# A two-block transformer step on one core: weight tiles split on VectorE alone, and TensorE multiplying zeros before its first inputs

## The chip, the cores and the metric

The kernel runs on one NeuronCore of a Trainium2 chip. The metric is the device time of one execution in microseconds (us). Five engines work side by side, each through its own queue in order: TensorE (PE in the profile; its weight loads are PEld), VectorE (DVE), ScalarE (ACT), GpSimd (POOL) and SyncE (SP, which here only starts transfers). DMA queues move data between HBM and the on-chip memory SBUF. TensorE writes to the accumulation memory PSUM.

## The reference

Two blocks follow one another on 256 rows of 1024 float32 values. All products are float32.

```python
# block 1
xn = rms_norm(x, norm1_g);  proj = xn @ w_in              # gates, keys, queries, values
mixed = concat(hgrn2_mixer(...), gla_mixer(...))          # two gated linear attentions
h = x + mixed @ w_out
h = h + peer_ffn(rms_norm(h, norm2_g), ...)               # 8 heads x 16 experts of 16384, gathered by row
x = rms_norm(h, norm_f_g)
# block 2
h = rms_norm(x, norm_pre);  cols = h @ w_in_2
ys = [deltanet(...), spatial_gating(...), sliding_window(...), memory(...)]
merged = sum(sigmoid(gate_n) * (ys[n] @ w_up[n]) for n in range(4))
out = x + rms_norm(merged @ w_out_2, norm_post)
```

## The kernel before

The 256 rows are two blocks of 128 partitions, handled as `b` = 0 and 1. The program is one long order written out in Python: generators yield between small steps, and `run`, `weave` and `pace` interleave them. Every engine then works through its own queue in the order in which the generators issued the instructions.

**Weights.** They come from HBM as tiles of 128 x 1024 float32 (512 KB), numbered `i`; four tiles make a group `g` of 512 output columns. `load_to` starts the transfers on SP in that order into `slot` tiles, of which there are 28 for all purposes. `wt(g, c)` loads some tiles ahead (`depth`) and cuts some tiles ahead (`ahead`) of the one that TensorE is about to use.

**Split products.** Most groups (`SPLIT`) are multiplied in three products of float32r halves (`mm3`, lines 365 to 367): high by high, high by low, low by high. So each tile is cut first (`cut`, lines 216 and 217): ScalarE casts it to the high half `hi`, then `lo = x - hi` is subtracted on VectorE or on Pool. Inputs are cut too, always on VectorE. The high and low halves lie in `pair` tiles (`wp`), of which there are 6 in the front and in the tail; a few of the last group are in `wh` and `wl`. `cut_to` chooses the engine of a weight tile: Pool if `state["pool"]` is set and `i % state["share"] == 0`, else VectorE; `share` is 2 at first, 3 in the front after the first inputs, 2 (`SHARE`) in the tail. Between front and tail `pool` is False.

**Stages.** In the front, `norm1` scales, transposes and cuts the input of both blocks (its steps are interleaved by hand with the cuts of the first four tiles), `bounds` computes small constants, and `front_chan`, `front_v` and `front_gate` project (hf, glow, hq, gq, gk, vg, g). `mixer_levels` works out the scores of the linear attention in seven levels on VectorE and TensorE (lv), woven between the projections; `mixer_out`, `peer_norm` and `first_scores` follow, and the first experts are selected. Then 256 gathers of 1 MB by Pool bring the experts' rows, VectorE and TensorE use them, and the rest of block 1 and a part of block 2 run in their shadow. In the tail, `tail_main` projects the second block's branches (zgm, zsw, zxm, zdn), gates and merges, while `pace` hands out the steps of `deltanet`, `sliding`, `spatial` and `memory_attn` between them; `finish` projects once more (o), normalizes and stores. L1468 and L1469 are the two VectorE operations of `merge`, L1190 and L1222 belong to the triangular solve of `deltanet`, L1353 to L1362 to the softmax of `sliding`.

**PSUM.** `bank` hands out accumulation tiles from rings of three, one ring ("pj") for projections and one ("ps") for the rest.

The edit touches `cut_to` and the hand-written order at the start:

```python
    n0, n1 = norm1(0), norm1(1)
    for g, n in ((n0, 0), (n1, 0), (n0, 0), (n1, 1), (n0, 1), (n1, 2), (n0, 3), (n1, 4)):
        next(g, None)
        cut_to(n)
```

Of the kernel before, what the change touches and what calls it, by code (L numbers as in the profile page):

```python
# [11 lines left out]
BF = mybir.dt.bfloat16  # L12
# [7 lines left out]
P = 128  # L20
# [7 lines left out]
N_SLOT, N_PAIR = 28, 6  # L28
N_EARLY, N_LATE = 8, 4
SLOT_US = 2.7  # L30
ZW = 7.0
SHARE, AH, LAST = 2, 2, 4
SC_OF = (0, 1, 2, 3, 4, 6, 5, 7)
LEVELS = (1, 2, 4, 8, 16, 32, 64)

# [22 lines left out]
def run(*gens):  # L58

    live = list(gens)  # L60
    while live:
        for g in list(live):
            try:
                next(g)
            except StopIteration:
                live.remove(g)
# [75 lines left out]
def kernel(ctx, tc, I, out, dbg=None):  # L142
    nc = tc.nc
    dbg = dbg or {}
    V, S, G, TE = nc.vector, nc.scalar, nc.gpsimd, nc.tensor
# [10 lines left out]
    def slot(name, dt=F32):  # L156

        return big.tile([P, 1024], dt, tag="slot", name=name)
# [11 lines left out]
    def pair(name, dt=F32):  # L170

        k = turn["at"] % turn["ring"]
        turn["at"] += 1
        return (pairs if k < N_PAIR else late["pairs"]).tile([P, 2048], dt, tag="pair", name=name)
# [19 lines left out]


    raw, parts = {}, {}
    state = {"next": 0, "cut": 0, "depth": 8, "ahead": N_PAIR - 2, "share": 2}

    def is_split(i):
        return any(4 * a <= i < 4 * b for a, b in SPLIT)  # L200

    def chunks(t):
        return t.rearrange("p (c n) -> p c n", c=2)
# [11 lines left out]
    def cut(x, hi, lo, eng=None):  # L215
        S.copy(hi, x)  # L216
        (eng or V).tensor_tensor(out=lo, in0=x, in1=hi.bitcast(F32), op=OP.subtract)  # L217

    def cut_to(n, eng=None):
        for i in range(state["cut"], min(n, state["next"])):  # L220
            if is_split(i):
                if i // 4 in (Z_GU, G_O2 + 1):
                    hi, lo = slot(f"wh{i}", F32R), slot(f"wl{i}", F32R)
                else:
                    wp = pair(f"wp{i}", F32R)
                    hi, lo = wp[:, :1024], wp[:, 1024:]
                cut(raw[i], hi, lo, eng or (G if state["pool"] and i % state["share"] == 0 else V))
                parts[i] = chunks(hi), chunks(lo)
        state["cut"] = max(state["cut"], min(n, state["next"]))

    def wt(g, c):
        i = 4 * g + c // 2
        load_to(i + 1 + state["depth"])
        cut_to(i + 1 + state["ahead"])
        return chunks(raw[i])[:, c % 2]
# [35 lines left out]
    S.activation(warm, one, AF.Exp)  # L271
    mhalf = cpool.tile([P, 1], F32, name="mhalf")
    V.memset(mhalf, -0.5)
    iota16 = cpool.tile([P, 16], BF, name="iota16")
    G.iota(iota16, pattern=[[1, 16]], base=0, channel_multiplier=0, allow_small_or_imprecise_dtypes=True)


    def bank(name, tag="pj"):
        return psum.tile([P, 512], F32, tag=tag, name=name)
# [4 lines left out]
    def small(name, *shape, dt=F32, bufs=2):  # L284
        return work.tile([P, *shape], dt, tag=name, name=name, bufs=bufs)
# [31 lines left out]
    def rstd2(ss):  # L317

        t = small("rst2", 2)
        V.tensor_scalar(t[:, 0:1], ss[:, 0:1], ss[:, 1:2], EPS, op0=OP.add, op1=OP.add)  # L320
        G.tensor_tensor(out=t[:, 1:2], in0=t[:, 0:1], in1=mhalf, op=OP.pow)
        return t[:, 1:2]

    def halves_rstd(x, junk, adds, meanwhile=lambda: None):

        ss = small("ssh", 2)
        for nh in range(2):
            s = slice(nh * 512, (nh + 1) * 512)
            adds[nh](s)
            S.activation(junk[:, s], x[:, s], AF.Square, scale=D ** -0.5, accum_out=ss[:, nh:nh + 1])  # L330
        r = rstd2(ss)
        meanwhile()
        return r

    def transposed(x, put, n=KC, scale=None):

        for h in range(n // 4):
            pt = bank4("pt")
            for c in range(4):
                cc = 4 * h + c  # L340
                if scale is None:
                    TE.transpose(pt[:, c], x[:, cc * P:(cc + 1) * P], ident)  # L342
                else:
                    TE.matmul(pt[:, c], x[:, cc * P:(cc + 1) * P], scale, start=True, stop=True)
            pe(1.1)
            yield
            put(h, pt)
        yield
# [10 lines left out]
    def gained(o, pt, gain, h):  # L359
        V.tensor_tensor(out=o, in0=pt, in1=gain[:, 4 * h:4 * h + 4, None].to_broadcast([P, 4, P]), op=OP.mult)  # L360
# [33 lines left out]
    def scaled(x, name):  # L394

        xs = slot(f"{name}_s")
        r = row_rstd(x, D, name, xs)
        V.tensor_scalar(xs, x, r, None, op0=OP.mult)
        return xs
# [6 lines left out]
    def norm1(b):  # L406
        tb = slice(b * P, (b + 1) * P)

        def put(h, pt):
            t = xT[b][:, 4 * h:4 * h + 4]  # L410
            if b == 0:
                gained(t, pt, chan[:, C_N1:C_N1 + 8], h)
            else:
                for c in range(4):
                    S.activation(t[:, c], pt[:, c], AF.Copy, scale=chan[:, C_N1 + 4 * h + c:C_N1 + 4 * h + c + 1])
            cut(t, xh[h][:, :, tb], xl[h][:, :, tb])

        xs = scaled(xr[b], f"n1{b}")
        yield
        yield from transposed(xs, put)  # L420
# [17 lines left out]
    def bounds():  # L438
        V.tensor_tensor(out=lb[:, 0], in0=l0, in1=l1, op=OP.max)
        V.tensor_tensor(out=lb[:, 1], in0=l0, in1=lb[:, 0], op=OP.subtract)  # L440
        V.tensor_tensor(out=lb[:, 2], in0=l1, in1=lb[:, 0], op=OP.subtract)
        S.activation(lb[:, 1:3], lb[:, 1:3], AF.Exp)
        V.tensor_tensor(out=lb[:, 3], in0=lb[:, 1], in1=lb[:, 2], op=OP.add)
        V.reciprocal(lb[:, 4], lb[:, 3])
        V.tensor_tensor(out=fb, in0=lb[:, 2], in1=lb[:, 4], op=OP.mult)
        V.tensor_scalar(fb, fb, 0.5, None, op0=OP.mult)
        V.tensor_tensor(out=fa, in0=lb[:, 1], in1=lb[:, 4], op=OP.mult)
        V.tensor_tensor(out=fa, in0=fa, in1=fb, op=OP.add)
        V.tensor_scalar(nfb, fb, -1.0, None, op0=OP.mult)
        cut(w_glow, gls[0], gls[1])  # L450
# [397 lines left out]
    def peer():  # L848
# [5 lines left out]
        for i in range(n + AHEAD[1] + LAG[1]):  # L854
# [38 lines left out]
            if n - 10 <= i < n - 2 and i % 2 == 0:  # L893
                cut_to(4 * Z_GU + 1 + (i - n + 10) // 2, V)
                load_to(4 * Z_GV + (i - n + 8) // 2)
# [28 lines left out]
    def last_out(b):  # L924

        x, junk, a, nf = xr[b], hn[b], acc[b], rowt["nf"]

        def add(s):
            V.tensor_tensor(out=x[:, s], in0=x[:, s], in1=a.rearrange("p a n -> p (a n)")[:, s], op=OP.add)

        def scale(s):
            V.scalar_tensor_tensor(x[:, s], x[:, s], r, nf[:, s], op0=OP.mult, op1=OP.mult)

        r = halves_rstd(x, junk, (add, add))
        yield
        r2 = halves_rstd(x, junk, (scale, scale))
        dump("x2", x, lambda d: d[b * P:(b + 1) * P])
        dr = small("dg", P, bufs=3)
        V.tensor_scalar(dr, ident, r2, None, op0=OP.mult)
        yield  # L940
        hT[b] = slot3(f"hT{b}", 8)
        hh2[b] = slot3(f"hh{b}", 8, P, F32R), slot3(f"hl{b}", 8, P, F32R)

        def put(h, pt):
            s = slice(4 * h, 4 * h + 4)
            gained(hT[b][:, s], pt, chan[:, C_NP:C_NP + 8], h)
            cut(hT[b][:, s], *[t[:, s] for t in hh2[b]])

        yield from transposed(x, put, scale=dr)
# [358 lines left out]
    def spatial_u(z, name, bs=range(NB)):  # L1308
        for b in bs:
            if (name, 0) not in B2:  # L1310
                B2[name, 0] = slot3(name, NB, 512)
            ps = yield from proj_tok(z, h2_of(b), "gm")
            S.activation(B2[name, 0][:, b], ps, AF.Gelu_apprx_tanh)
            B2[name, "of", b] = B2[name, 0]
            yield
# [190 lines left out]


    n0, n1 = norm1(0), norm1(1)
    for g, n in ((n0, 0), (n1, 0), (n0, 0), (n1, 1), (n0, 1), (n1, 2), (n0, 3), (n1, 4)):
        next(g, None)  # L1510
        cut_to(n)
    run(n0, n1)
    bounds()
    state.update(ahead=3, share=3)
    run(front_chan())

    half_gains = rows[:, :R_AL].rearrange("p (a b) -> p a b", b=P)
# [88 lines left out]


    rowt["gm"] = slot("row_gm")[:, :512]
    state["share"] = SHARE

    more_weights()
    state["ahead"] = -1
    lo, sp = last_out(1), spatial_u(Z_GU, "gmu", [0])
# [130 lines left out]
```

## Time and profile before

| | |
|---|---|
| three timed runs, median | 1228.71 us (1226.76 to 1230.31) |
| the profiled execution | 1228.49 us |
| its span, first to last instruction | 1226.4 us |
| TensorE busy (PE) | 1065.2 us, 87% |
| VectorE busy (DVE) | 889.3 us, 73% |
| ScalarE busy (ACT) | 505.0 us, 41% |
| Pool busy | 450.1 us, 37% |
| mean granted TensorE clock | 0.946 |

The times in the profile are microseconds from the span's start. A busy engine is not always one that advances: an operation that stands still for another counts as busy, and so does a matrix product at half clock. So the shares are read beside the length of single instructions (compare the shortest, the median and the longest of one form) and beside the idle time before an instruction, whose releaser stands in brackets behind it. The granted clock of a stretch is 1.00 at 2.4 GHz and 0.50 at 1.2 GHz.

### The profile page before, as it was taken

The numbers are of one execution on the slowest core, as the hardware profiler recorded it, in microseconds if no ns is written. First come the engines' busy times: TensorE is split into PE (matmuls) and PEld (weight loads), VectorE is DVE, ScalarE is ACT, GpSimd is POOL, SyncE is SP. The second block draws the span as 40 slices with busy tenths as digits, with TensorE's granted clock in tenths as the row PEclk, the third lists the DMA queues.
The fourth block names the chain that finished last, engine by engine and source line by source line (L and its number), as shares of the span: only waits on it lengthen the run. The fifth ranks groups of instructions, "written<-read, shape, count | busy, mean of one in ns | idle before, by whom it ended". The sixth has DMA issues, their size and how long they took to land. (4 is left out here: it accounts for less than half of the span.)

```text
span 1226.4 us, 14725 instructions
## 1 busy us (share of the span) xinstructions
PE 1065.2 (87%) x4938; PEld 732.8 (60%) x4938; DVE 889.3 (73%) x1825; ACT 505.0 (41%) x1267; POOL 450.1 (37%) x328
## 2 busy tenths in 40 slices
PE   6999969888979886978888888887799999999897
PEld 6876635445437653624555445544379878887775
DVE  5588677886588678889889899865737576456654
ACT  5615234442333342434344734547343524344342
POOL 3313224344335343443444454652120323244542
PEclk9998989989989998988889889998999989999999
DMA  9625489999999999999999999999546543345630
GB/s 366 216 88 201 164 366 363 374 365 378 425 428 424 425 421 427 424 426 426 425 425 425 401 413 427 426 427 361 199 162 238 210 138 120 118 140 172 199 109 34
DMA packets 68074, 376.38 MB, mean 307 GB/s; under 512 B 7696, under 2 KB 8992, under 8 KB 35232
## 3 DMA queue, kind: packets, MB, share of 16 engines
q0 software_dynamic: 36864, 268.45, 53.1%
q1 hardware_dynamic: 29264, 103.56, 23.6%
q10 hardware_dynamic: 1872, 3.44, 0.8%
q8 instruction: 39, 0.64, 0.2%
q14 instruction: 35, 0.29, 0.1%
HBM read 374.38 MB, written 1.05 MB: 306 GB/s over the span
## 5 line engine op out<-in xcount | busy, mean ns | idle before, releaser
L886 PE MATMUL acc<-uv,dg 128*128 128x512 f32 x836 | 426.7, 647 | 105.4 <-ACT dg L874 99.6
L835 POOL DMA_INDIRECT uv<-in_peer_uv_dram,idx x256 | 303.8, 1187 | 428.0 <-PE acc L886 259.4
L863 DVE SCALAR_TENSOR_TENSOR uv<-uv,hn 128x1024 f32<-128x1024 f32 x256 | 307.6, 1220 | 76.8 <-DMA uv<-in_peer_uv_dram,idx 73.4
L886 PEld LDWEIGHTS acc<-uv,dg 128*128 128x128 f32 x836 | 159.2, 205 | 288.7 <-issue 144.3
L217 POOL TENSOR_TENSOR wp<-w,wp 128x1024 fp32r<-128x1024 f32 x48 | 128.6, 2689 | 265.8 <-ACT wp L216 265.2
L867 ACT ACTIVATE ge<-act 128x1 f32<-128x1 f32 x256 | 51.8, 202 | 378.8 <-DVE uv L863 367.8
L217 DVE TENSOR_TENSOR wp<-w,wp 128x1024 fp32r<-128x1024 f32 x60 | 108.9, 1828 | 78.8 <-ACT wp L216 78.8
L216 ACT CAST wp<-w 128x1024 fp32r<-128x1024 f32 x108 | 107.4, 1049 | 18.5 <-PE hq L367 8.7
L874 ACT ACTIVATE dg<-mats,wv 128x128 f32<-128x128 f32 x209 | 81.3, 389 | 1.4
L868 ACT ACTIVATE wv<-ge,gw 128x1 f32<-128x1 f32 x256 | 75.4, 295 | 8.3
L391 PEld LDWEIGHTS pq<-hnT,w 128*128 128x128 f32 x512 | 60.5, 192 | 9.8 <-issue 8.8
L880 DVE SCALAR_TENSOR_TENSOR x<-uv,wv,x 128x1024 f32<-128x1024 f32 x47 | 60.2, 1281 | 2.7 <-ACT wv L868 2.5
L391 PE MATMUL pq<-hnT,w 128*128 128x128 f32 x512 | 61.5, 276 | 0.6 <-DVE hnT L354 0.6
L366 PE MATMUL gate<-wp,hh 128*128 128x512 f32 x128 | 51.2, 400 | 6.0 <-DVE wp L217 3.5
L365 PE MATMUL gate<-wp,hh 128*128 128x512 f32 x128 | 52.0, 406 | 0.0
L367 PE MATMUL gate<-wp,hl 128*128 128x512 f32 x128 | 50.6, 395 | 0.0
L391 PEld LDWEIGHTS qkv<-hT,w 128*128 128x128 f32 x384 | 46.5, 197 | 6.8 <-issue 6.6
L391 PE MATMUL qkv<-hT,w 128*128 128x128 f32 x384 | 46.5, 279 | 0.0
L366 PEld LDWEIGHTS gate<-wp,hh 128*128 128x128 f32 x128 | 24.4, 190 | 12.7 <-DVE wp L217 4.3
L1449 ACT ACTIVATE gate<-gate 128x512 f32<-128x512 f32 x16 | 9.6, 598 | 53.6 <-PE gate L367 53.6
L1042 DVE SCALAR_TENSOR_TENSOR qkvT<-qkvr,chan,qkvT 128x128 f32<-128x128 f32 x72 | 24.1, 352 | 5.7 <-ACT qkvT L1040 4.0
L367 PEld LDWEIGHTS gate<-wp,hl 128*128 128x128 f32 x128 | 24.5, 191 | 5.1
(500 smaller groups left out, 1825.6 us busy)
## 6 DMA issues: line engine op xcount, KB each, us to landing
w<-in_wts_dram SPq DMA_DIRECT2D x188, 512.0 KB, 4.7
uv<-in_peer_uv_dram,idx POOLq DMA_INDIRECT x256, 12.4
wsm<-in_w_small_dram ACTq DMA_DIRECT2D x8, 132.0 KB, 19.5
x<-in_x_dram SPq DMA_DIRECT2D x2, 512.0 KB, 4.8
skT<-in_skT_dram ACTq DMA_DIRECT2D x2, 512.0 KB, 9.1
mem<-in_mem_dram SPq DMA_DIRECT2D x2, 512.0 KB, 9.3
out_dram<-o SPq DMA_DIRECT2D x4, 256.0 KB, 2.0
row_n<-in_gains_dram ACTq DMA_DIRECT2D x1, 512.0 KB, 4.0
```

The lines of the kernel that those rows point to most:

```text
L216: S.copy(hi, x)
L217: (eng or V).tensor_tensor(out=lo, in0=x, in1=hi.bitcast(F32), op=OP.subtract)
L365: TE.matmul(ps, fh, sh, start=start, stop=False)
L366: TE.matmul(ps, fh, sl, start=False, stop=False)
L367: TE.matmul(ps, fl, sh, start=False, stop=stop)
L391: TE.matmul(ps, wt(g, c)[:, s], x, start=c == 0, stop=c == KC - 1)
L835: G.indirect_dma_start(out=t, out_offset=None, in_=I["peer_uv"], in_offset=bass.IndirectOffsetOnAxis(ap=idx[b][:, h, s:s + 1], axis=0))
L863: V.scalar_tensor_tensor(t, t, 1.0, hn[b], op0=OP.mult, op1=OP.mult, accum_out=act[:, h, s:s + 1])
L868: S.activation(wv[dots], ge, AF.Copy, scale=gw[b][:, h, s:s + 1])
L874: S.activation(dg[diags], ident, AF.Copy, scale=wv[diags])
L880: V.scalar_tensor_tensor(xr[b], t, wv[sums], xr[b], op0=OP.mult, op1=OP.add)
L886: TE.matmul(acc[b][:, nh], dg[sums], t[:, nh * 512:(nh + 1) * 512], start=start, stop=h == 7 and s == 15)
```

## The change

`cut_to` gives every weight tile's subtraction to VectorE unless an engine is named; `share`, its two settings and the constants `SHARE` and `AH` go. A new tile `zeros` (128 x 512 bfloat16 in one of the 28 slots) is cleared on VectorE. A new function `spin(n)` issues `n` products of zeros, 128 columns of weights by 512 columns, into a PSUM tile that nobody reads. It is called with 18 before the first transposes are issued, and with 8 after each of the two steps of the hand-written order that have `n` = 1: between the transposes of the second block's first half, of the first block's second half and of the second block's second half.

```diff
-SHARE, AH, LAST = 2, 2, 4
+LAST = 4
...
-    state = {"next": 0, "cut": 0, "depth": 8, "ahead": N_PAIR - 2, "share": 2}
+    state = {"next": 0, "cut": 0, "depth": 8, "ahead": N_PAIR - 2}
...
-                cut(raw[i], hi, lo, eng or (G if state["pool"] and i % state["share"] == 0 else V))
+                cut(raw[i], hi, lo, eng or V)
...
+    zeros = slot("zeros", BF)[:, :512]
+    V.memset(zeros, 0.0)
...
+    def spin(n):
+
+        ps = bank("spin")
+        for _ in range(n):
+            TE.matmul(ps, zeros[:, :P], zeros, start=True, stop=True)
...
     n0, n1 = norm1(0), norm1(1)
+    spin(18)
     for g, n in ((n0, 0), (n1, 0), (n0, 0), (n1, 1), (n0, 1), (n1, 2), (n0, 3), (n1, 4)):
         next(g, None)
         cut_to(n)
+        if n == 1:
+            spin(8)
     run(n0, n1)
     bounds()
-    state.update(ahead=3, share=3)
+    state["ahead"] = 3
...
-    state["share"] = SHARE
```

## Rows read from the trace of the kernel before

**Rows 1.** The page: its first line, and the Pool group of cuts.

```profile
span 1226.4 us, 14725 instructions
...
L217 POOL TENSOR_TENSOR wp<-w,wp 128x1024 fp32r<-128x1024 f32 x48 | 128.6, 2689 | 265.8 <-ACT wp L216 265.2
```

**Rows 2.** Windows: stretch, busy us by engine, PE clock, DMA share, GB/s.

```profile
118.00:146.00 28.00, 27.15 (x142) 20.83 (x141) 17.28 (x41) 10.40 (x21) 3.24 (x2) 0.94 0.48 165
200.00:800.00 600.00, 511.24 (x2067) 299.87 (x2066) 494.36 (x1197) 240.96 (x761) 259.14 (x218) 0.93 1.00 414
```

**Rows 3.** Line 217 from 884 us: count, shortest/median/longest ns, first and last start.

```profile
L217 DVE TENSOR_TENSOR wp<-w,wp x36: 1207/2172/3411, 897.9 to 1197.5; 128x1024 fp32r<-128x1024 f32 x36
```

**Rows 4.** VectorE's groups from 884 us: busy us, mean ns, idle before.

```profile
L217 DVE TENSOR_TENSOR wp<-w,wp 128x1024 fp32r<-128x1024 f32 x36 | 71.4, 1989 | 64.0 <-ACT wp L216 64.0
L1469 DVE TENSOR_TENSOR mg<-mg,gate 128x512 f32<-128x512 f32 x12 | 18.6, 1554 | 0.4
...
L1156 DVE TENSOR_SCALAR rsb<-rsb 128x4 f32<-128x4 f32 x1 | 2.4, 2352 | 0.0
```

**Rows 5.** TensorE's waits from 884 us: who for whom, us, times, longest.

```profile
PE gate L366 <- DVE wp L217: 3.5, 2, 2.0
PE swt L1380 <- DVE L L1175: 3.0, 1, 3.0
PE gate L366 <- POOL wp L217: 2.5, 3, 1.1
...
PE mt L1424 <- ACT msc L1420: 1.2, 1, 1.2
```

**Rows 6.** Timeline near 903 us: start, length, instruction, idle before and releaser.

```profile
901.66 2.37 POOL L217 TENSOR_TENSOR wp<-w,wp 128x1024 fp32r<-128x1024 f32 x1 [2.30 <-ACT wp L216]
...
904.08 0.50 PE L366 MATMUL gm<-wp,hh 128*128 128x512 f32 x1 [1.13 <-POOL wp L217]
```

**Rows 7.** Timeline of TensorE at the start.

```profile
10.31 2.82 PE L342 MATMUL pt<-mats,n_s 128*128 128x128 f32 x12 [1.92 <-DVE n_s L398]
...
13.30 0.58 PE L365 MATMUL hf<-xh,wp 128*128 128x256 f32 x1 [0.17 <-ACT xh L216]
...
14.62 0.41 PE L365 MATMUL hf<-xh,wp 128*128 128x256 f32 x1
...
14.84 0.41 PE L366 MATMUL hf<-xl,wp 128*128 128x256 f32 x1
...
22.88 0.28 PE L367 MATMUL hf<-xh,wp 128*128 128x256 f32 x1
...
23.00 0.28 PE L365 MATMUL hf<-xh,wp 128*128 128x256 f32 x1
...
33.71 0.38 PE L367 MATMUL hq<-xh,wp 128*128 128x256 f32 x1 [0.75 <-DVE wp L217]
```

**Rows 8.** Timeline of VectorE and TensorE, 77 to 115 us.

```profile
77.43 2.61 DVE L621 TENSOR_TENSOR f<-f 128x384 f32<-128x384 f32 x1
...
82.59 1.96 PE L597 MATMUL lv<-ql,kl 128*128 128x64 f32 x16 [1.28 <-DVE sc L604]
...
106.24 4.53 DVE L217 TENSOR_TENSOR wp<-w,wp 128x1024 fp32r<-128x1024 f32 x2
...
114.93 1.12 PE L342 MATMUL pt<-mats,mix 128*128 128x128 f32 x4 [2.46 <-DVE mix L692]
```

**Rows 9.** Windows after three of TensorE's waits; the granted clock is third from the end.

```profile
85.00:86.00 1.00, 1.00 (x4) 0.73 (x3) 1.00 (x4) 0.00 (x0) 0.00 (x0) 0.50 0.00 0
...
114.00:116.00 2.00, 1.07 (x4) 0.72 (x4) 1.66 (x5) 0.00 (x0) 1.39 (x1) 0.64 1.02 416
...
987.00:990.00 3.00, 3.00 (x10) 2.31 (x10) 1.27 (x2) 0.29 (x1) 0.00 (x0) 0.50 1.01 366
```

**Rows 10.** Timeline near 966 us: ScalarE's exponential, and TensorE's next start.

```profile
965.44 0.21 ACT L1362 ACTIVATE sw_es<-sw_es 128x8 f32<-128x8 f32 x1 [2.54 <-DVE sw_es L1360]
...
967.90 0.50 PE L366 MATMUL zgm<-wp,hh 128*128 128x512 f32 x1 [0.77 <-DVE wp L217]
```

## The prediction

> **What bounds the kernel now.** I read the page, then the windows by stage, then TensorE's waits, then the timeline at each wait. The profiled execution took 1228.49 us, of which the span is 1226.4 [rows 1]; the 2.1 us outside it I leave as they are. The median of the three timed runs is 1228.71, so the profile stands for it. There are three stages. The front (to 146 us) and the tail (from 884 us) multiply split weights, and TensorE sets their time: it is busy nearly throughout and each of its gaps has a named releaser. The gathers in between (146 to 884) are bound by DMA, whose engines are 1.00 busy from 200 to 800 us [rows 2]. That stage takes what it takes once it has begun, so a microsecond saved in the front starts it a microsecond earlier and is kept.
>
> In front and tail a weight tile goes ACT cast, then subtraction on VectorE or Pool, then TensorE. Pool's subtraction takes 2.37 us [rows 6], VectorE's alone 1.21 us; but VectorE's own median in the tail is 2.17 us and its worst 3.41 [rows 3]. Next to a Pool subtraction VectorE stands still: an operation on 128x4 elements took 2.35 us, and L1469 averages 1.55 us [rows 4] where its shortest takes 0.69. So a Pool cut hurts twice: its own tile is late, and VectorE is late.
>
> **Part 1: 50 cuts move to VectorE** (48 pairs [rows 1] and two of the last group: 12 in the front, 38 in the tail). Each adds 1.21 us to VectorE and takes away the standstill it caused. In the tail that standstill, from the groups by line (mean less the shortest, times count), is 36 x 0.78 = 28 us on VectorE's own cuts, 12 x 0.86 = 10 on L1469 [rows 3, 4] and 19 on eight smaller groups, in all 57 us over 38 cuts: 1.5 us relieved for 1.21 added. From 40 to 135 us the same count gives 14 us for 8 cuts. VectorE's work thus falls by some 11 us in the tail and 4 in the middle of the front. On Pool's queue only memsets, powers and the gathers stand behind the cuts and begin no later; the slots that SP's loads wait for come free with the end of a cut, about 1.2 us earlier where that was Pool's: nothing. What the move does to TensorE goes wait by wait.
>
> *Waits for a Pool cut in the tail.* TensorE needs a group's third tile a fixed time after the last activation of the group before, and ACT casts it only behind that activation; the subtraction is then on the path. At 904.08 the wait was 1.13 us [rows 6]; four more of 1.1 to 1.2 us are of that kind (two of the three of gate [rows 5], one of up, one of o) and one of 0.24. A cut 1.16 us shorter ends them: five at 1.0 us and 0.2, **-5.2 us**. Two others of the kind don't gain. At 965 us the maximum of the sliding window's scores stands behind the cut on VectorE, and ACT's next cast behind its exponential (965.44); with 1.2 us more on VectorE that cast comes 0.75 us later, so TensorE, which resumed at 967.90 [rows 10], resumes at 968.6: **+0.7**. At 1019 us a cut comes before the triangular solve's update on VectorE, for which TensorE waits in order: **+0.3** (-0.7 to +0.8).
>
> *Waits for a late VectorE in the tail.* swt 3.0 us, mt 1.2 and two of gate, 1.4 and 2.0 [rows 5]. In each I replace the stalled durations by the free ones and put the moved cuts in. Before swt: 2.75, 2.34 and 1.21 become 0.69, 0.17, 1.21 and one or two cuts of 1.21: -2.2. Before mt: 2.87 + 2.87 become 4.3 with two cuts and L1190, the wait goes: -1.1. Before gate at 1123: 4.0 of stalls for 3.6 of cuts: -0.4. Before gate at 1159: 6.5 of stalls and late starts for 4.8 of cuts: -1.6. After the first and the last of these the clock was at 0.50 for some 3.5 us [rows 9], that is 1.7 us lost each time; with gaps of 0.8 and 0.4 us I take two thirds as saved: -2.2. Sum **-7.5** (-3 to -10).
>
> *Levels of the mixer, 58 to 96 us.* VectorE's product took 2.61 us instead of 0.56 beside a Pool cut, and TensorE waited 1.28 us for the scores [rows 8], then ran at half clock [rows 9] for six wide matmuls at 0.43 instead of 0.23 us. Four cuts (4.8 us) replace 7.0 us of stalls, so VectorE is 2 us ahead and the wait, two smaller ones (0.5 in sum) and most of the half clock go: **-2.8** (-1 to -3.3).
>
> *First mixer output.* TensorE waited 2.46 us at 114.93 behind VectorE, whose two cuts at 106.24 took 4.53 us [rows 8]. Three cuts (3.6 us) replace 5.0 us of stalls and a late start: -1.9; a half clock followed here too [rows 9], 1.8 us, of which I take 1.0: **-2.9** (-1 to -4).
>
> *New waits.* VectorE and ACT work strictly in order. A cut that Pool ran ahead now stands in VectorE's queue before a product that TensorE waits for. The trace of before doesn't show this; from below it costs nothing (VectorE's sum falls), from above 1.21 us for each of the six or so places from 1040 to 1120 us where a chain of small products runs between the gates: 0 to +7, I take **+2**, nearer to nothing because stalls of 1.5 us stood at the same places without a wait.
>
> **Part 2: the start.** hf starts at 13.30 at half clock, 0.22 us from matmul to matmul, and later 0.12 [rows 7]; 25 of 96 are slow, 2.4 us. The trace has no zero multiplication; the nearest rows, wide matmuls, come every 0.43 us at half and 0.23 at full clock. The first 18 begin after a memset (near 1.3 us) and end by 9.1 at the latest, before anything needs the transposes. The two times 8 stand in TensorE's queue between the transposes, the first of which can't run before 10.31 [rows 7]: hf then can't begin before 15.7 us at full clock (three transposes at 0.6, 16 x 0.23). Meanwhile the first tile's cut now stands on VectorE ahead of the gain of the transposed input: +1.2 us on that chain, less 0.8 of standstill that goes, and likewise for the third tile. Followed operation by operation, hf's last inputs are there at 21.35 instead of 20.7, hf ends at 27.1 instead of 27.6, and VectorE, with a seventh tile to cut ahead of f and k, delivers hq's fourth tile at 33.85, for which TensorE waited until 33.71 [rows 7]: **+0.2**. So VectorE decides the start and the faster clock is not collected.
>
> The Trainium skill ("TensorE: Matmul & The Clock Gate", section "What's actually happening") says that the array's default is the throttled clock and that activity releases it. By that alone hf would gain its 2.4 us and the sum be 2.6 lower; it is a rival below.
>
> The zeros take a 28th part of the slots until about 15 us; one weight load then starts later, 20 us ahead of its use: nothing.
>
> **Sum:** -5.2 + 0.7 + 0.3 - 7.5 - 2.8 - 2.9 + 2 + 0.2 = **-15.2 us**, from 1228.5 to **1213.3**.
>
> **The rivals.**
> A. The sum: 1213.3, by its bounds 1208 to 1219. For it speaks that every term has a releaser's row.
> B. VectorE's queue eats the gain: the new waits at their upper end (+7) and half of the late-VectorE terms lost (+4): some 1222. For it: the stretch at 965 us.
> C. Slower: the standstill isn't given back, because something else made VectorE's durations long. Eighteen moved cuts lie in the six stretches where VectorE decides (4, 3, 2, 2, 3, 4). With a relief of r each, they cost 18 x (1.21 - r); with -5.2 for the Pool waits and 3.2 of other costs it turns slower below r of 1.1. At r = 0.5: 12.8 + 3.2 - 5.2 = +10.8, 1239. Against it: the 1.5 us counted above, and none of VectorE's long durations in the tail lies away from a Pool span.
> D. The zeros run at half clock and hold the start: TensorE is idle for about 2 us between the 18 and 10.31 us, and after the 2.46 us before 114.93 the clock was 0.64 and then half [rows 8, 9]. Then 16 x 0.43 and slow transposes put hf at 20.4 and everything behind it by +3.9: 1217. The same page names idleness as what throttles again, which is on this rival's side.
> E. The start collects the clock: -2.4 there, 1211, if VectorE's chain is shorter than I made it.
> F. The gathers swallow the front's 5.5 us, for instance because loads that ran before them now run among them: 1219. Against it: DMA's share was 0.48 just before them [rows 2].
>
> **How the numbers follow.** A 0.55, B 0.15, C 0.08, D 0.10, E 0.05, F 0.07. The time is A's. The range goes from 1206 (A with its upper clock terms) to 1223 (B, D, F inside, C out). About 0.3%, 3.7 us, is what a measurement can tell: faster 0.85 (all but C and the weak end of B), same 0.07, slower 0.08.
>
> **What would show it.** Pool's L217 rows gone and VectorE's all near 1.21 us; VectorE busy some 13 us less than before in spite of 50 more cuts; no wait of TensorE for Pool; the gaps at 82.59 and 114.93 closed; the first gather some 5 us earlier; hq's wait still there. I am wrong if VectorE's cuts stay near 2 us (C), if TensorE's waits for VectorE in the tail exceed 8 us (B), or if hf starts after 18 us (D).

## The result and the profile after

The changed kernel takes 1206.24 us (median of four runs, 1206.16 to 1207.49) against 1227.74 us for the kernel before: a ratio of 0.9824, 95% interval 0.9802 to 0.9845, or 21.5 us less. I had forecast 15.2 us less. The profiled execution took 1206.16 us, against 1228.49 before, with this page (its first line, then the cuts: count, busy us and mean ns, idle before and releaser):

```profile
span 1204.4 us, 14791 instructions
...
L217 DVE TENSOR_TENSOR wp<-w,wp 128x1024 fp32r<-128x1024 f32 x108 | 127.8, 1219 | 77.8 <-ACT wp L216 77.8
```

Pool's group of cuts [rows 1] is gone, and VectorE's mean is 1.22 us, about its shortest before (1.21). The stretch from 875 us says the same by line, first as shortest/median/longest ns, then by groups:

```profile
L217 DVE TENSOR_TENSOR wp<-w,wp x72: 1194/1218/1227, 888.8 to 1177.3; 128x1024 fp32r<-128x1024 f32 x72
...
L217 DVE TENSOR_TENSOR wp<-w,wp 128x1024 fp32r<-128x1024 f32 x72 | 85.3, 1219 | 65.7 <-ACT wp L216 65.7
...
L1477 DVE TENSOR_TENSOR mg<-mg,gate 128x512 f32<-128x512 f32 x12 | 8.3, 692 | 0.4
```

72 cuts cost VectorE 85.3 us where 36 had cost 71.4, and the product that is now L1477 went from 18.6 to 8.3 us [rows 3, 4]. Over the whole kernel the page has VectorE at 873.4 us; before it had 889.3. With 50 cuts of 1.21 us added, the standstill that went is, by this estimate, 15.9 + 60.5 = 76.4 us, 1.53 us for each cut moved.

TensorE's waits from 875 to 1205 us (who for whom, us, times, longest):

```profile
PE zgm L373 <- ACT wp L216: 2.1, 1, 2.1
PE pt L352 <- DVE dg L947: 1.2, 1, 1.2
PE zgm L374 <- DVE wp L217: 0.8, 1, 0.8
PE pt L350 <- ACT L L1193: 0.7, 1, 0.7
PE gm L373 <- ACT hh L216: 0.5, 1, 0.5
PE zdn L374 <- DVE wp L217: 0.4, 1, 0.4
```

Of the list of before [rows 5] swt, mt, both kinds of gate, up and o are gone; new are the first row, at zgm, and the fourth, a pt behind swt. The levels and the first mixer output, in windows (stretch, its length, then busy us of PE, PEld, DVE, ACT and POOL with counts; granted clock, DMA share, GB/s):

```profile
58.00:96.00 38.00, 37.98 (x237) 32.04 (x236) 32.54 (x63) 11.99 (x15) 0.00 (x0) 1.00 0.33 117
96.00:118.00 22.00, 20.81 (x96) 15.86 (x96) 20.25 (x26) 12.12 (x16) 2.40 (x2) 1.00 0.68 241
```

TensorE has no gap left in the levels, and the clock, 0.50 and 0.64 in places before [rows 9], stays at 1.00. Before the first mixer output TensorE waits twice, once for each half of pt. The second wait of the kernel before, behind the 2.46 us of [rows 8], and then both of the changed kernel:

```profile
116.62 1.09 PE L342 MATMUL pt<-mats,mix 128*128 128x128 f32 x4 [0.57 <-DVE mix L692]
```

```profile
108.62 0.66 PE L350 MATMUL pt<-mats,mix 128*128 128x128 f32 x4 [0.16 <-DVE mix L700]
110.31 0.63 PE L350 MATMUL pt<-mats,mix 128*128 128x128 f32 x4 [1.03 <-DVE mix L700]
```

Their sum fell from 3.03 to 1.19 us.

**Where the 22 us lie.** I compared the first and last instruction of each of TensorE's tiles in the two timelines; a shift that changes between two tiles arose between them.

| place (times of before) | forecast | measured |
|---|---|---|
| start, to the end of hq at 44 | +0.2 | -0.2 |
| levels, to the end of vg at 96 | -2.8 | -3.6 |
| first mixer output, to the end of wo at 130 | -2.9 | -4.4 |
| gathers, to 884 | 0 | +0.1 |
| Pool wait at 904 | -1.0 | -1.1 |
| small products and xmq, 947 to 961 | 0 | +3.2 |
| zgm, 961 to 977 | +0.7 | +2.2 |
| swt at 986 and the clock behind it | -3.3 | -4.9 |
| zdn at 1020 | +0.3 | -0.3 |
| mt at 1041 | -1.1 | -1.3 |
| chains between the gates, to 1095 | +2 | 0 |
| gate, up and o, 1098 to 1220 | -7.3 | -11.8 |
| sum | -15.2 | -22.1 |

### The profile page after: what moved, and what is told of

Its sections match the earlier page's. It is cut to its first block, busy times and chain, and to the rows that moved or that the text cites. A ratio compares the mean times of both kernels' runs of the same rounds, so it can differ in the third digit from the quotient of the medians.

```text
span 1204.4 us, 14791 instructions
## 1 busy us (share of the span) xinstructions
PE 1067.0 (89%) x4972; PEld 732.5 (61%) x4972; DVE 873.4 (73%) x1876; ACT 505.2 (42%) x1267; POOL 311.6 (26%) x278
## 4 chain that ended last, share of the span: by engine, by line
PE 43%; DVE 25%; DMA 14%; ACT 7%; issue 7%; POOL 3%; ACTq 0%; POOLq 0%; DVEq 0%; SPq 0%
DMA uv<-in_peer_uv_dram,idx 12%; DVE uv L871 10%; PE acc L894 7%; POOL uv L843 3%; PE pq L399 3%; PE gate L374 2%; PE gate L373 2%; PE gate L375 2%; DVE x L888 2%; PE qkv L399 2%; PE lv L605 2%; PE xmq L399 1%; DVE ti L754 1%; PE up L374 1%; PE up L375 1%
## 5 line engine op out<-in xcount | busy, mean ns | idle before, releaser
L843 POOL DMA_INDIRECT uv<-in_peer_uv_dram,idx x256 | 298.3, 1165 | 433.6 <-PE acc L894 266.3
L871 DVE SCALAR_TENSOR_TENSOR uv<-uv,hn 128x1024 f32<-128x1024 f32 x256 | 307.8, 1220 | 78.0 <-DMA uv<-in_peer_uv_dram,idx 70.7
L217 DVE TENSOR_TENSOR wp<-w,wp 128x1024 fp32r<-128x1024 f32 x108 | 127.8, 1219 | 77.8 <-ACT wp L216 77.8
L295 POOL TENSOR_TENSOR rsb<-rsa,mhalf 128x1 f32<-128x1 f32 (+2 forms) x8 | 7.3, 909 | 291.9 <-DVE rsa L292 291.9
L399 PEld LDWEIGHTS pq<-hnT,w 128*128 128x128 f32 x512 | 60.5, 192 | 9.0 <-issue 8.8
L323 POOL TENSOR_TENSOR rst<-rst,mhalf 128x1 f32<-128x1 f32 x5 | 2.8, 559 | 144.1 <-DVE rst L322 144.1
```

What stands on the lines that cost most here:

```text
L399: TE.matmul(ps, wt(g, c)[:, s], x, start=c == 0, stop=c == KC - 1)
L843: G.indirect_dma_start(out=t, out_offset=None, in_=I["peer_uv"], in_offset=bass.IndirectOffsetOnAxis(ap=idx[b][:, h, s:s + 1], axis=0))
L871: V.scalar_tensor_tensor(t, t, 1.0, hn[b], op0=OP.mult, op1=OP.mult, accum_out=act[:, h, s:s + 1])
```

## Experiments

The theory: the gain is the end of VectorE's standstill beside Pool's subtractions, and of the late tiles that Pool delivered; the zeros bring nothing, since VectorE's chain to hq decides the start. Rivals: the zeros carry part of the gain; the standstill has another cause than Pool; the two losses near 943 and 961 us belong to the cuts. e1, e2, e4 and e5 ran on one chip (kernel before 1228.90 us), e3, e6, e7 and e8 on a second (1227.34), e4b, e9 and e0 on a third (1228.60). Only kernels of one chip are compared to within a few microseconds.

### One part at a time: e1 and e2

e1 is the changed kernel without zeros and their products, e2 the kernel before with them.

```diff
-    zeros = slot("zeros", BF)[:, :512]
-    V.memset(zeros, 0.0)
...
-    spin(18)
...
-        if n == 1:
-            spin(8)
```

> All cuts on VectorE, no zero matrix products (the other half of the change left out). If VectorE's chain decides the start, the zeros bring next to nothing: hf runs slowly for its first 25 products, ends about 27.5 instead of 26.4 us, hq waits less than 1.6 us for its fourth tile and goes on at 33.5 to 34.0; 1206 to 1207 us. If the zeros carry a good part of the gain beyond the forecast (the clock of hf, 2.4 us, and what follows from it), 1208.5 us or more.

> The zero matrix products alone, cuts shared with Pool as before. If VectorE's chain decides the start: hf at full clock, its end before 27 us, but a longer wait of hq, so no difference beyond 1 us (1227 to 1228). If the clock of hf is worth its 2.4 us: 1225.

e1: 1205.08 us, ratio 0.9796 (0.9770 to 0.9823). e2: 1229.10 us, ratio 1.0001 (0.9982 to 1.0021). The cuts alone give the whole gain, and the zeros none that the times can tell (the interval of e2 is 2 to 3 us wide to either side). Why, the timeline of TensorE shows; first e1, then the changed kernel (start, length, instruction, idle before):

```profile
13.97 0.58 PE L371 MATMUL hf<-xh,wp 128*128 128x256 f32 x1 [1.22 <-ACT xh L216]
...
33.79 0.39 PE L373 MATMUL hq<-xh,wp 128*128 128x256 f32 x1 [1.07 <-DVE wp L217]
```

```profile
1.24 5.51 PE L330 MATMUL spin<-zeros 128*128 128x512 bf16 x18 [1.24 <-DVE zeros L275]
...
10.11 1.89 PE L330 MATMUL spin<-zeros 128*128 128x512 bf16 x8
...
14.35 0.36 PE L373 MATMUL hf<-xh,wp 128*128 128x256 f32 x1
14.55 0.28 PE L374 MATMUL hf<-xl,wp 128*128 128x256 f32 x1
14.67 0.28 PE L375 MATMUL hf<-xh,wp 128*128 128x256 f32 x1
...
33.52 0.39 PE L375 MATMUL hq<-xh,wp 128*128 128x256 f32 x1 [1.60 <-DVE wp L217]
```

With the zeros hf runs at full clock from its first products (0.12 us from one to the next) and ends at 26.42 instead of 27.60. But hq then waits 1.60 instead of 1.07 us for VectorE and resumes 0.27 us earlier, not 1.18. In e2 likewise: hf ends 1.38 us earlier, vg begins 0.38 earlier, and by the last gather nothing is left (+0.05). e2's profiled span is 2.4 us short all the same; that arises behind swt and gate, where the clock came back sooner, and the timed runs don't show it.

### Fewer zeros: e3

```diff
-        if n == 1:
-            spin(8)
```

> The changed kernel without the two times 8 zero products, with the 18 before the transposes. A look at the clock and the start. If the 18 alone keep the clock: hf begins near 13.7 us, as soon as its inputs are there, and runs at 0.12 us a product. If the idle 1.9 us before 9.6 throttle TensorE without the two times 8: hf runs at 0.21 for its first products as in the kernel before. Either way hq goes on at about 33.5 us, and the time is that of the changed kernel within 1 us.

One run: 1201.53 us. hf begins 0.8 us earlier than in the changed kernel, ends 1.0 later because part of it ran at half clock (0.64 granted from 16 to 20 us), and gq begins 0.16 earlier. So the two times 8 keep hf at full clock and delay its start, and at gq neither is left.

### Where the start's gain is stuck: e4, e8, e4b

In all three the weight tiles of the start are begun four ahead of TensorE instead of three; in e8 the zeros are left out as well.

```diff
-    state["ahead"] = 3
+    state["ahead"] = 4
```

> The changed kernel with four instead of three tiles cut ahead in the first projection, so that the fourth tile of hq is cut before the 16 small VectorE operations on f and k instead of behind them. If the clock gained at the start is lost in the 1.6 us wait of hq for that tile: the wait goes and about 1.4 us are gained, 1204.8. If something behind it takes the time instead (VectorE later in the levels): 1206.2 as the changed kernel.

> Four tiles cut ahead, all cuts on VectorE, no zero products. If the zeros are worth their clock as soon as hq doesn't wait for its fourth tile: hf ends near 27.6 us instead of 26.6, and vg begins 1.0 to 1.3 us later than with zeros and four ahead (54.6 us). If they are worth nothing even then: vg begins at 54.6.

> The changed kernel with the weight tiles begun four ahead instead of three, a second time, so that it stands beside the next kernel and the changed kernel on one chip. If the order of VectorE at hq is what took the start's gain, it stays some 1 to 3 us under the changed kernel. If its lower time of the first run was the chip of that call, it is equal to it within 1 us.

e4 took 1203.19 us (0.9788, 0.9762 to 0.9815), e8 1201.91 (0.9797, 0.9766 to 0.9828), e4b 1205.24 (0.9809, 0.9796 to 0.9823) beside 1205.76 for the changed kernel on its chip. In e4's trace hq no longer waits and gq begins 2.06 us earlier than in the changed kernel; in e8 hf ends 1.32 us later than in e4 and vg begins 1.32 us later. So it was VectorE's order at hq that kept the clock's gain from arriving. In the time this is hardly to be seen: e4 is 1.9 us under e1, e4b 0.5 us under its neighbour, with overlapping intervals, less than I expected. One reason is in e4b's trace: its hf began only at 16.96 us, 2.6 us later than in the changed kernel's profile, and it gained nothing at gq (+0.05):

```profile
10.54 0.66 PE L350 MATMUL pt<-mats,n_s 128*128 128x128 f32 x4 [2.64 <-DVE n_s L406]
11.03 2.92 PE L330 MATMUL spin<-zeros 128*128 128x512 bf16 x8
...
14.60 2.17 PE L330 MATMUL spin<-zeros 128*128 128x512 bf16 x8
...
16.96 0.36 PE L373 MATMUL hf<-xh,wp 128*128 128x256 f32 x1
```

Of the 2.6 us only 0.9 is the scaled input, which reached the transposes at 10.54 instead of 9.61 us. The rest is mostly the zeros themselves: part of the two times 8 ran at half clock (2.92 and 2.17 us instead of 1.89 each), and hf stood behind them in TensorE's queue, though ScalarE had its first input ready at 14.56 us. The changed kernel run again (e0, below) shows the same, with its hf at 16.38:

```profile
10.45 3.23 PE L330 MATMUL spin<-zeros 128*128 128x512 bf16 x8
```

So in two of the nine profiled executions with the two times 8 the zeros did what rival D says, in part.

### Is it Pool that holds VectorE? e5

VectorE makes every cut as in the changed kernel; Pool subtracts its former tiles once more, in four pieces, into a scratch tile that nobody reads. Which tiles these are follows `share` as in the kernel before.

```diff
+                if eng is None and state["pool"] and i % state["share"] == 0:
+                    S.copy(hi, raw[i])
...
+                    for q in range(4):
+                        s = slice(256 * q, 256 * (q + 1))
+                        G.tensor_tensor(out=waste, in0=raw[i][:, s], in1=hi.bitcast(F32)[:, s], op=OP.subtract)
+                    V.tensor_tensor(out=lo, in0=raw[i], in1=hi.bitcast(F32), op=OP.subtract)
...
```

> The changed kernel, but for each tile that was Pool's before, Pool subtracts as well, in four pieces, into a small tile that nobody reads; VectorE does all cuts that count. No weight waits for Pool. If Pool's subtraction is what makes VectorE stand still: VectorE's cuts go back to a mean of 1.9 us or more, its busy time grows by 60 us or so, TensorE waits for VectorE as in the kernel before and more, 1225 to 1245 us. If VectorE's long durations had another cause: cuts stay at 1.22 us, 1206 to 1208.

It took 1239.27 us: 1.0073 of the kernel before (1.0045 to 1.0102), and 34 us more than e1 on the same chip. No product reads what Pool computes there, but not all of the 34 us is VectorE's standstill: Pool's queue is longer too, and others wait for it. Two of these waits, both in the front (who for whom, us, times, longest):

```profile
DVE ql L632 <- POOL ql L592: 4.5, 1, 4.5
ACT wp L228 <- POOL cand L232: 1.8, 1, 1.8
```

The first is VectorE's for a memset that stands behind Pool's pieces, the second ScalarE's for a buffer that they still read. By line, Pool's pieces and VectorE's cuts of the same tiles (shortest/median/longest ns):

```profile
L232 POOL TENSOR_TENSOR cand<-w,wp x192: 722/1242/2947, 9.5 to 1209.9; 128x256 f32<-128x256 f32 x192
...
L233 DVE TENSOR_TENSOR wp<-w,wp x48: 1204/1688/1775, 9.5 to 1209.2; 128x1024 fp32r<-128x1024 f32 x48
```

VectorE's longest cut is 1.775 us, 0.56 over its 1.21. A whole subtraction takes Pool 2.37 us [rows 6], so a quarter is some 0.59 us, an estimate: VectorE's standstill in one cut is about as long as one Pool instruction at most. With Pool's whole tiles the longest was 3.41 [rows 3], 2.2 over. Pool itself stands still too: 1.24 us for a quarter in the median, 4.9 for a tile. The Trainium skill ("SBUF — State Buffer", section "Who interferes with whom") says that a VectorE instruction with two SBUF inputs and a GpSimd instruction that reads SBUF take turns at a shared pair of ports, held for the whole instruction; the trace agrees, in both directions.

This is the slower rival's mechanism (C) with its condition made to hold. The page of e5 has VectorE at 922.9 us, 49.3 more than e1's 873.6 with the same cuts on it: that is the standstill which Pool's pieces cause. Against the kernel before it is 33.6 us more, with 50 cuts more on it: the relief is 1.21 - 33.6/50 = 0.54 us a cut. My formula gave 1239 at 0.5, and 1239.27 was measured. That they agree so closely is luck, since the formula has nothing for Pool's longer queue and has 2 us for new waits that the changed kernel did not show; I take it as support for the sign, no more. I had expected a mean cut of 1.9 us or more; it was 1.55, because Pool's work was cut into quarters.

### The two losses near 943 and 961 us: e6, e7, e9, e0

e6 gives one tile back to Pool, the third of zgm's group (number 118). e9 does so with the tiles four ahead, and e0 is the changed kernel again, on e9's chip. e7 puts wide products between the one-column products near 941 us (nobody reads their results).

```diff
-                cut(raw[i], hi, lo, eng or V)
+                cut(raw[i], hi, lo, eng or (G if i == 4 * Z_GZ + 2 else V))
```

```diff
+        junk = mats.rearrange("p a b -> p (a b)").bitcast(BF)
...
+            if b:
+                TE.matmul(ps[:, 1:4], junk[:, :P], junk[:, :3 * P].rearrange("p (a b) -> p a b", b=P), start=True, stop=True)
```

> The changed kernel with one tile, the third of zgm's group, back on Pool. If that cut on VectorE ahead of the sliding window's maximum is what makes ACT's next cast late: the exponential comes 1.2 us earlier against its group's first product, TensorE's waits of 2.1 and 0.8 us become about 1.1, 0.2 and 0.8 as before, 0.7 us are gained, and up to 1.5 us more if the half clock behind the wait goes. If the wait has another cause (the transfer, the softmax itself): no difference or 1.1 us more.

> The changed kernel with eight products of 384 columns (of a constant, read by nobody) put between the 8 one-column products of l2p in the tail. In the profile of the changed kernel TensorE went to half clock at 943 us without any wait, behind l2p, own and prev, and lost 3.2 us there. If the small products are what lets the clock fall: it stays at 1.00 from 940 to 950, 3.2 us are gained for 1.3 us of added products, net -1 to -2. If it falls for another reason: +1.3.

> The changed kernel with the tiles begun four ahead and the one tile ahead of the 2.1 us wait of zgm subtracted on Pool. If that wait is VectorE's queue, Pool takes 1.2 us of cut out of it and the half clock behind it goes: 1 to 4 us under the kernel with four ahead alone. If the wait is ScalarE's cast, it is equal to that kernel, or up to 1 us slower by the standstill of one Pool subtraction.

> The changed kernel itself, on the chip of this call, as the measure for the two kernels beside it: 1204 to 1208 us.

e6: 1201.79 us, ratio 0.9794 (0.9757 to 0.9832). e7: 1205.51, 0.9826 (0.9791 to 0.9860). e9: **1200.26**, 0.9780 (0.9767 to 0.9793). e0: 1205.76, 0.9826 (0.9810 to 0.9842). So e9 beats both kernels: it stands 5.5 us under the changed kernel and 5.0 us under e4b on the same chip, more than the 1 to 4 I expected, and the intervals of the two ratios don't touch. In the two profiles 4.6 us lie between them, 3.4 of it at zgm; the other 1.2 was there before the last gather, where this tile plays no part (e4b's late start).

zgm in the changed kernel, and in e9:

```profile
961.21 0.50 PE L373 MATMUL zgm<-wp,hh 128*128 128x512 f32 x1 [2.12 <-ACT wp L216]
...
962.47 0.50 PE L374 MATMUL zgm<-wp,hh 128*128 128x512 f32 x1 [0.76 <-DVE wp L217]
```

```profile
950.72 2.38 POOL L217 TENSOR_TENSOR wp<-w,wp 128x1024 fp32r<-128x1024 f32 x1 [6.22 <-ACT wp L216]
...
953.15 0.50 PE L374 MATMUL zgm<-wp,hh 128*128 128x512 f32 x1 [1.09 <-POOL wp L217]
```

and the windows around these waits, first of the changed kernel, then of e9:

```profile
944.00:948.00 4.00, 4.00 (x19) 3.77 (x19) 1.68 (x3) 0.20 (x1) 1.65 (x1) 0.50 0.77 247
...
960.00:964.00 4.00, 2.04 (x6) 1.44 (x7) 2.57 (x4) 3.81 (x8) 0.00 (x0) 0.92 0.63 220
964.00:968.00 4.00, 4.00 (x19) 3.58 (x18) 3.40 (x5) 2.90 (x13) 0.00 (x0) 0.66 0.87 292
```

```profile
944.00:948.00 4.00, 4.00 (x34) 3.76 (x34) 0.00 (x0) 0.00 (x0) 0.50 (x1) 1.00 0.31 111
...
952.00:956.00 4.00, 1.98 (x7) 1.05 (x6) 2.72 (x6) 2.33 (x5) 1.09 (x1) 1.00 0.92 362
956.00:960.00 4.00, 3.87 (x23) 3.40 (x23) 3.69 (x7) 3.89 (x16) 0.00 (x0) 1.00 0.69 216
```

Behind the one wait of 2.1 us the clock falls to half for a while (0.92 and 0.66 in the windows); behind three short ones (1.09, 0.29 and 0.77 us) it doesn't. From the timelines of all kernels, the time from the first product of xmq to the first of zgm, and from there to zgm's end:

| kernel | xmq to zgm, us | zgm, us |
|---|---|---|
| before | 13.10 | 16.02 |
| changed | 16.31 | 18.24 |
| e0, the same again | 14.72 | 18.22 |
| e1 | 16.31 | 18.27 |
| e2, cuts as before | 13.10 | 16.00 |
| e3 | 13.09 | 17.99 |
| e4, e4b | 13.09, 13.09 | 19.30, 19.45 |
| e5, Pool's cuts made twice | 14.68 | 19.96 |
| e7 | 13.78 | 18.25 |
| e8 | 13.09 | 18.04 |
| e6, one tile on Pool | 14.72 | 16.01 |
| e9, one tile on Pool | 13.09 | 16.01 |

zgm's loss belongs to the cuts: it is there in every kernel that doesn't take the low half of this tile from Pool (2.0 to 3.9 us) and in none that does. The other loss does not belong to them as such. It is a half clock that is there in some profiles and not in others with the same tail (e1 and e8), and that cost the same kernel 3.2 us once and 1.6 the other time; none of these products waits. e7 had none, and paid 0.7 us for its added products; but e3, e4, e4b, e8 and e9 had none either without them, so e7 decides nothing. (Its profile also lost 1.7 us elsewhere: behind hq's wait of 1.6 us its clock was 0.50 from 35 to 37 us, where the changed kernel's stayed at 1.00 behind the same wait.) What sets it off stays open.

## Why the prediction was right, and where it was off

The time was inside the range by 0.24 us, at its lower edge, and that much is luck: the sum's own bounds were 1208 to 1219, two of e0's five executions of the same kernel lay below the range (1203.14 and 1203.90), and without 4.7 us of loss at xmq and zgm that no step had, the profiled time would have been 1201.5. The mechanism was the forecast one: the Pool waits that I had priced went (five of them, 1.13 to 1.22 us each and wholly, where I had allowed 1.0), VectorE's cuts are all near 1.21 us, and its busy time fell by 15.9 us for a forecast of 13. By the steps:

- **The start** was right, and so was its reason (VectorE decides: forecast +0.2, measured -0.2; hq resumed at 33.52, forecast 33.85). e1 and e2 put the zeros at nothing that can be told, and e4 shows where their gain stops. One step was off: hf began at 14.35, where I had called 15.7 the earliest; 0.7 of it is that the second block's transposes began at 9.61 instead of 10.31. Rival D did not come in this profile (eight zero products took 1.89 us, full clock), but in e0 and e4b it did in part. The price there was small: with hf 2.0 us later, e0's gq began 0.37 us later than in the changed kernel's profile, because VectorE still decides. With four tiles ahead, where hq doesn't wait, e4b's gq began 2.1 us later than e4's. Rival E fell with e1.
- **The front's gain is kept:** the gathers began 8.2 and ended 8.1 us earlier; F is out.
- **Late VectorE in the tail** was the mis-sized term: -7.5 in the sum, some -13 measured (swt 4.9, mt 1.3, and the 11.8 of gate, up and o less 4.9 of waits for Pool and the one of 0.24). Near 1123 us I set 4.0 us of stalls against 3.6 us of cuts and left 1.0 us of wait. The stalls I counted were those of three products; I had left out that of the cut ahead of them, the first of these two rows of VectorE in the kernel before:

```profile
1109.03 2.77 DVE L217 TENSOR_TENSOR wp<-w,wp 128x1024 fp32r<-128x1024 f32 x1 [0.57 <-ACT wp L216]
...
1112.44 2.19 DVE L1469 TENSOR_TENSOR mg<-mg,gate 128x512 f32<-128x512 f32 x1
```

  That cut alone stalled 1.56 us; with it 5.6 us stand against 3.6, and the wait of 1.4 goes wholly, as it did. At 1161 the whole 2.03 went instead of 1.6, and with it all of the half clock behind it.
- **swt and its clock:** -4.9 for -3.3. I took the middle between one and two cuts in the chain's place and saved two thirds of the clock. The changed kernel's VectorE there shows two cuts for one, and still no wait:

```profile
974.69 0.69 DVE L1304 TENSOR_TENSOR yb<-yb,zgm_t 128x512 f32<-128x512 f32 x1
975.30 1.22 DVE L217 TENSOR_TENSOR wp<-w,wp 128x1024 fp32r<-128x1024 f32 x1
976.43 0.17 DVE L1378 TENSOR_TENSOR sw_su<-sw_su,sw_es 128x8 f32<-128x8 f32 x1
...
976.75 1.22 DVE L217 TENSOR_TENSOR wp<-w,wp 128x1024 fp32r<-128x1024 f32 x1
977.89 1.12 DVE L1183 SCALAR_TENSOR_TENSOR L<-kk,dg_r,dd 128x128 f32<-128x128 f32 x4
```

  From the first of these to the end of the last it takes 4.3 us, where it took 7.4. With the gap the half clock behind it went too, and whole, where I had saved two thirds of it.
- **Levels and first mixer output:** -3.6 and -4.4 for -2.8 and -2.9, for the same reason. At the first mixer output the two waits fell by 1.84 us (3.03 to 1.19), as forecast (1.9); the other 2.5 of the 4.4 is mostly matmuls that no longer run at half clock, of which I had taken 1.0.
- **New waits behind the moved cuts:** +2 forecast, none seen. Behind the 0.4 us at 1011.13, which were 0.7 before, TensorE has no gap over 0.15 us to the end of o; the one new wait ahead of that, zgm apart, 0.7 us at 982 for ScalarE, is in swt's -4.9. Rival B is out except for one place.
- **That place is zgm.** My +0.7 was right as far as it went: the waits there were 2.15 us before and are 2.88. What I missed is that three short waits become one of 2.1, behind which the clock halves: 1.5 us more. e6 and e9 take both away with one tile.
- **+3.2 at xmq** was in no step. The moved cuts alone don't bring it: e4, e4b and e8 have them, with the same tail, and lost nothing there, and e0, the same kernel, lost half. What does stays open.

So the gain was 7 us larger in the profiles than forecast (22.1 for 15.2) because I undersized what follows from a freed VectorE (by 9.7 us, the small terms included) and priced new waits that didn't come (2), against 4.7 us of half clock and of waits at zgm that I hadn't foreseen.

## What to carry to other kernels

Here Pool and VectorE subtracted side by side from SBUF, and sharing the work cost more than it gave. In such a kernel compare VectorE's mean with its shortest duration per line, and include the shared operation itself in the stalls you count. Then look for the one place where a cut stands in VectorE's queue ahead of a chain that ScalarE and TensorE wait for; leaving that single tile on Pool was worth 2.2 us in e6's trace and 3.4 in e9's, which has the lowest ratio of all. A warmed clock pays only where nothing else comes due at the same time: here VectorE's fourth tile did. And work put into a queue to warm the clock stands ahead of what matters, and can run at half clock itself, as in e0 and e4b.

## What the runs showed of the hardware that I had not expected

- The granted clock fell to 0.50 near 943 us, behind one-column and 64-partition products, with TensorE at 4.00 of 4.00 us busy and no wait. In five of the twelve profiled executions of the table above (the kernel before left out) it cost 1.6 or 3.2 us; seven ran without it.
- VectorE's standstill in one cut follows the length of one Pool instruction: up to 2.2 us beside whole subtractions, up to 0.56 us beside quarters.
- The eighteen zero products that begin at 1.24 us took 5.5 us: the first eight came 0.43 us apart, the others 0.22, so the clock rose while they ran. hf's products still came 0.12 us apart from the first, in spite of a gap of 1.92 us before the transposes at 9.61 us. Where that gap was 2.24 us (e0) and 2.64 us (e4b), zero products behind it came 0.43 us apart again.
